# A block of the first layer's out projection for token half 0 set between half 1's products and its last rows, with gate and y rows moved four tiles at a time

## The chip, the core and the metric

The kernel runs on one core of one Trainium2 chip. The metric is device time in microseconds, as a median of several executions. PE is the matrix engine (TensorE), DVE, ACT and POOL are the vector, scalar and GpSimd engines, and SP is the engine that here issues every DMA, one after the other, from one queue. Each engine works through its own list in order; waits between engines go through semaphores.

## What is computed

Two decoder layers over 1024 tokens of width 1024 with 16 heads of 64. The first mixes with forgetting attention (FoX), the second with dilated windows. Cut to what bears on the change:

```python
for i in range(2):
    h = rms_norm(x, norm_g[i])
    if i == 0:
        o, gate = fox_mixer(h, w_in, b_f, q_g, k_g)
    else:
        o, gate = dsw_mixer(h, cos, sin, w_in, q_g, k_g)
    x = x + (o * silu(gate)) @ w_out
```

`fox_mixer` projects `h` to q, k, v, gate and forget logits, and runs causal softmax attention with the running sum of the log forget gates added to the scores. `cos` and `sin` are the rotary tables of the second layer.

## The kernel before

Every large product is made of three fp16 products (high by high, high by low, low by high), so operands exist as a high and a low part: `xh`, `xl` for the normed rows, and in the same buffers `yh`, `yl` for the gated attention output.

**The FoX stage.** After the first layer's gates (`gates`, stored row by row in DRAM as `gs_d`) come eight head pairs, `hp` 0 to 7. For each, `project` (L694) makes q, k and v of eight token tiles `t`, and `fox_tile` queues for every tile: scores on PE (L870), a biased minimum on DVE (L1125), exp on ACT (L913), a low part on POOL (L919), a transposing DMA from `ph` to `ptt` (L920), and the products with v on PE (`pv`, L927 to L929). At a tile's end DVE multiplies by the reciprocal sum and by the gate: two instructions (L1158) that read the gate slice `gsf`, loaded by its own 64 KB DMA for each tile (L1106), and write the tile `y`. For `hp` 0 to 6 a DMA writes `y` to `y_d` (L1162). For the last pair `turn_last` transposes `y` on PE right away (L729), and ACT and DVE split the result into `yh` and `yl` (L734, L735). The rows of the earlier pairs come back from `y_d` in the last pair's time and are turned by `turn_y`.

**The out projection.** `project_t` (L719) multiplies by `w_out` with the weights stationary and 512 tokens (a token half `b`) moving. The 1024 output columns are cut into three weight blocks `h` of 384, 256 and 384 columns, that is 3, 2 and 3 output blocks `m` of 128. One output block takes 24 products: 8 row blocks `k` by 3. For `h` = 0 the order over `k` is 0 to 3, then 4 to 6, then 7, over all three `m`, since `k` = 7 is the last head pair, whose rows come late. The order is: both halves of `h` = 0, then half 0 with `h` = 1 and 2, then half 1 with `h` = 1 and 2. Output blocks wait in three PSUM buffers of `ps_pj` (tile `pj`); three others (`ps_s`, tag `s`) hold scores and transposes.

**What follows an output block.** `grown` loads the old rows (`xr`, L1239), adds the product on DVE (L1241, which frees the PSUM buffer), writes the sum to `x1_d` (L1242), scales by the next norm's gain on ACT (L1244), writes that to `xn_d` (L1245), and adds the squares up (L1247 to L1254). After the eighth block of a half, `factors` makes the row factor: a product `so` on PE (L1262), then `fv` and `fy` on DVE and ACT. `take` loads the rows again (`xs`, L1272); DVE multiplies by `fy` (L1275), ACT casts to `xh` (L1279), and DVE or POOL makes `xl` (L1280). The second layer's gates (`gates`, `project` at L694) read `xh` and `xl`, half 0 first; they load the next weights through `Weights` (`raw`, L619; bound L629 and L631; scale from the product `ws`, L601; split L659 and L660).

**What sets the order.** `Flow` counts ticks as products are written and calls what is due. Then `order_engines` plans all engines' lists from estimated durations and fixes each list; an engine never leaves its list. So a small edit can move instructions in places that it doesn't name. Tiles of one tag share a set number of buffers (`CFG`): `n2k` has 3, for `xr`, the gates' `ge` and a few others, `gsl` 3, `qs` 5. `rotary_tables` (L531 to L570, on DVE and ACT) is due 14 ticks after the first `project_t`.

Of the kernel before, what the change touches and what calls it, by code (L numbers as in the profile page):

```python
# [11 lines left out]
F32 = mybir.dt.float32  # L12
# [5 lines left out]
ALU = mybir.AluOpType  # L18
# [419 lines left out]
def trunk(ctx, tc, ins, out, cfg):  # L438
# [31 lines left out]
    def lay(shape, dtype, name, tag):  # L470
        return layer["pool"].tile(shape, dtype, name=name, tag=tag, bufs=layer["bufs"][tag])
# [138 lines left out]
    class Weights:  # L610
# [87 lines left out]

    def project_t(seq, done):

        under["ps"] = None
        todo = []
        for b, h in seq:
            n = PARTS[h][1] // P
            ms = [[m] for m in range(n)] if h else [list(range(n))]
            for mm in ms:
                for ks in [range(KT)] if h else [range(4), range(4, KT - 1), range(KT - 1, KT)]:
                    todo.extend((b, h, m, k) for m in mm for k in ks)
        n, s0 = 4 * NT * len({h for _, h in seq}), flow.now
        ps, ws = {}, {}  # L710
        for i, (b, h, m, k) in enumerate(todo):
            if h == 0:
                assert all((t, (k > 3) + (k > 6)) in turned for t in range(4 * b, 4 * b + 4)), (b, k, turned)
            if h not in ws:
                ws[h] = next_block(*cfg["out"][len(seq) > 2, len(ws)])
            if k == 0:
                ps[m] = ps_pj.tile([P, 512], F32, name="pj", tag="pj")
            for x, (j, a) in enumerate(((0, yh), (0, yl), (1, yh))):
                nc.tensor.matmul(ps[m], ws[h].slab(k, j)[:, m * P : (m + 1) * P], a[:, k, 512 * b : 512 * (b + 1)], start=(k == 0 and x == 0), stop=(k == KT - 1 and x == 2))  # L719
# [365 lines left out]
    def load_bc(hp, h, es=(0, 1)):  # L1085
        for e in es:
            bcs[hp, e, h] = lay([P, 5 * P], F32, name="bc", tag="ga")
            nc.sync.dma_start(bcs[hp, e, h][:, P:], c_d[2 * hp + e, h * 512 : (h + 1) * 512].partition_broadcast(P))

    def fox_tile(hp, t, kts, vt, sl):  # L1090
        LP = cfg["lpf"]
# [60 lines left out]
        def finish():  # L1152
            o = st["o"]
            rec = sm.tile([P, 2], F32, name="rec", tag="rec")
            nc.vector.reciprocal(rec, o[:, :, HD])
            y = sb.tile([P, P], F32, name="y", tag="y")
            for e in range(2):
                nc.vector.scalar_tensor_tensor(y[:, e * HD : (e + 1) * HD], o[:, e, :HD], rec[:, e : e + 1], st["gs"][:, e * HD : (e + 1) * HD], ALU.mult, ALU.mult)  # L1158
            if hp == NHP - 1:
                turn_last(y, t, flow.now + 3, 0)  # L1160
            else:
                nc.sync.dma_start(y_d[t * P : (t + 1) * P, hp * P : (hp + 1) * P], y)  # L1162


# [346 lines left out]

CFG = dict(out={(False, 0): (), (True, 0): ((18, 20, 22, 24), (0, 0, 1, 1), 3, (4, 6, 8, 10)), (True, 1): ((18, 20, 22, 24), (14, 15, 17, 18), 24, (33, 35, 37, 39))}, take=(((33, 34, 37, 40), 42), ((62, 63, 66, 69), 71)), rush=2000, gate=(((6, 7, 8, 9), (0, 0, 1, 1), 4, (5, 6, 7, 9)), ((44, 45, 46, 47), (26, 28, 30, 32), 36, (38, 40, 42, 44)), ()), bc=((1, 0, 26), (1, 1, 28), (0, 0, 38), (0, 1, 46)), wpool=3, rbufs=8, most=(0, 2), lcm=7, ps=0, pv=100, ph_=100, ph=1, wbufs=8, pl=3, um=3, lpf=8, lsd=((16, 16), (16, 14), (14, 11)), ty2=((0, 4), (1, 5)), hb=2, ub=2, qb=1, nb=3, fox=(((0, 0, 2, 2), (2, 4)), ((0, 0), (4, 4))), due=(29, 33, 39, 45, 35, 41, 49, 57), l1=dict(ga=8, ptt=4, ph=3, p=4, qk_t=6, qs=5, vt=3, gsl=3), l2=dict(ga=4, cmb=4, gsd=4, ptt=3, ph=3, p=2, qk_t=3, og=3, vt=3, gsl=3, par=1), wload=(18, 20, 22, 24), wbound=(0, 1, 3, 4), wscale=8, wsplit=(10, 16, 22, 12))

# [51 lines left out]
```

## Time and profile before

| what | value |
|---|---|
| median of 3 runs | 1655.86 us (1652.52 to 1656.51) |
| profiled execution | 1656.83 us, of which the span is 1654.8 us |
| FoX, first score read by DVE to last y | 142.4 to 531.4 us |
| first layer's out projection | 479.2 to 591.9 us, between other work up to 532 us |
| second layer's gates begin | 591.87 us |

A row of the timeline gives start, duration, engine, line, operation, output and inputs; in brackets stands how long the engine had been idle before it, and who released it. A row of the waits gives who waited for whom, the sum in us, how often, and the longest. A row of the windows gives a stretch, its length, busy time and instructions of each engine, then the granted PE clock as a share of full speed, the share of DMA time, and GB/s.

### The profile page before, as it was taken

To read this page: it belongs to the slowest core of one execution; us is meant where nothing else is said; L and a number is where in the kernel's file an instruction comes from. 1 tells how busy PE (TensorE), PEld (TensorE's weight loads), DVE (VectorE), ACT (ScalarE), POOL (GpSimd) and SP (SyncE) were. 2 spreads that over 40 slices of the span, in tenths; PEclk is the share of its full clock that TensorE was granted. 3 is DMA by queue.
4 is the path that set the end of the run, shared out by engine and by line. 5 is a ranking of instruction groups with operands and counts; after the bars stand their busy time and mean duration, and the time that the engine had idled before them with its cause. 6 is when DMAs were issued, how large, how long until landed. Compare 5 with 4: busy or idle time off the path is not lost.

```text
span 1654.8 us, 37873 instructions
## 1 busy us (share of the span) xinstructions
PE 1605.9 (97%) x13342; PEld 1037.5 (63%) x13342; DVE 1192.6 (72%) x3663; ACT 1063.5 (64%) x2746; POOL 963.9 (58%) x1252
## 2 busy tenths in 40 slices
PE   6999999999998999999999999999999999999999
PEld 4766667777664456566666666666666666666644
DVE  7757878888786586576767787777677877768751
ACT  7656778878776476566766687566566665666630
POOL 7315778778765241255555666667576766858430
PEclk9999999999999999999999999999999999999999
DMA  7335999999999884257876796768787586767952
GB/s 257 127 107 121 205 205 216 203 208 197 206 220 218 237 250 153 85 138 151 168 150 149 164 227 147 174 158 181 160 164 165 141 191 155 170 160 167 219 166 96
DMA packets 646479, 288.66 MB, mean 174 GB/s; under 512 B 493825, under 2 KB 610561, under 8 KB 646289
## 3 DMA queue, kind: packets, MB, share of 16 engines
q1 hardware_dynamic: 646288, 286.25, 74.5%
q8 instruction: 104, 1.70, 0.4%
q14 instruction: 87, 0.70, 0.1%
HBM read 124.35 MB, written 41.22 MB: 100 GB/s over the span
## 4 chain that ended last, share of the span: by engine, by line
PE 74%; DVE 10%; DMA 6%; ACT 4%; issue 3%; POOL 2%; SPq 0%; DVEq 0%; POOLq 0%; ACTq 0%
PE pj L694 56%; PE pj L719 7%; PE s L870 6%; DMA qk_t<-hl 3%; DVE w L660 2%; DVE p L1125 1%; PE ob L929 1%; PE ob L927 1%; PE ob L928 1%; DMA ptt<-ph 1%; ACT w L659 1%; PE o L929 1%; PE o L927 1%; PE o L928 1%; DVE xl L1280 1%
## 5 line engine op out<-in xcount | busy, mean ns | idle before, releaser
L694 PE MATMUL pj<-w,xh 128*128 128x384 f16 (+2 forms) x4864 | 1172.9, 324 | 6.0 <-DVE peak L904 4.3
L694 PE MATMUL pj<-w,xl 128*128 128x384 f16 (+2 forms) x2432 | 787.8, 324 | 5.2 <-DVE xl L1280 3.6
L694 PEld LDWEIGHTS <-xh 128*128 128x128 f16 x4864 | 468.1, 98 | 282.2 <-issue 8.2
L694 PEld LDWEIGHTS <-xl 128*128 128x128 f16 x2432 | 238.2, 98 | 157.5 <-DVE xl L1280 5.3
L1363 POOL TENSOR_TENSOR ph<-p,ph 128x768 f16<-128x768 f32 (+2 forms) x96 | 157.7, 1642 | 137.6 <-ACT ph L1362 130.1
L919 POOL TENSOR_TENSOR ph<-p,ph 128x512 f16<-128x512 f32 (+3 forms) x176 | 173.0, 1003 | 56.9 <-issue 37.5
L837 POOL TENSOR_TENSOR hl<-u,hl 128x512 f16<-128x512 f32 x128 | 150.9, 1179 | 53.6 <-ACT hl L836 44.9
L719 PE MATMUL pj<-xh,w 128*128 128x512 f16 x512 | 157.7, 381 | 6.2 <-DVE xr L1241 2.8
L870 PE MATMUL s<-qk_t 128*128 128x128 f16 (+1 forms) x1248 | 151.2, 238 | 6.8 <-DMA qk_t<-hl 5.1
L660 DVE SCALAR_TENSOR_TENSOR w<-raw,sws,w 128x768 f16<-128x768 f32 x96 | 146.6, 1528 | 11.0 <-ACT w L659 10.7
L794 ACT ACTIVATE sq<-pj 128x256 f32<-128x256 f32 x256 | 96.4, 377 | 86.5 <-DVE u L789 85.7
L789 DVE TENSOR_TENSOR u<-pj,gr 128x256 f32<-128x256 f32 x256 | 106.9, 418 | 45.8 <-PE pj L694 44.0
L913 ACT ACTIVATE p<-p,acc 128x512 f32<-128x512 f32 (+2 forms) x192 | 110.0, 608 | 38.0 <-DVE acc L1125 37.5
L719 PEld LDWEIGHTS <-w 128*128 128x128 f16 x768 | 74.5, 98 | 89.5 <-issue 9.2
L1352 ACT ACTIVATE p<-p,og 128x128 f32<-128x128 f32 (+1 forms) x256 | 104.1, 442 | 27.3 <-DVE og L1350 26.2
L927 PEld LDWEIGHTS <-ptt 128*128 128x128 f16 x1136 | 105.9, 98 | 19.8 <-DMA ptt<-ph 7.9
L928 PEld LDWEIGHTS <-ptt 128*128 128x128 f16 x1136 | 105.2, 96 | 11.4
L629 ACT ACTIVATE jk<-raw 128x768 f16<-128x768 f32 (+2 forms) x88 | 72.2, 820 | 62.5 <-DMA raw<-in_w_dsw 38.7
L821 POOL TENSOR_TENSOR ra<-u,cs 128x128 f32<-128x128 f32 x96 | 44.8, 467 | 108.5 <-DVE u L789 106.6
L1350 DVE CUSTOM_DVE_ANT_0 p<-s,band 128x256 f32<-128x256 f32 (+1 forms) x256 | 90.7, 373 | 22.8 <-PE s L870 22.6
L836 ACT CAST hl<-u 128x512 f16<-128x512 f32 x128 | 78.7, 614 | 42.5 <-DVE u L834 40.2
L929 PEld LDWEIGHTS <-ptt 128*128 128x128 f16 x1136 | 105.4, 97 | 0.0
(211 smaller groups left out, 3017.1 us busy)
## 6 DMA issues: line engine op xcount, KB each, us to landing
raw<-in_w_dsw SPq DMA_DIRECT2D x96, 384.0 KB, 4.2
raw<-in_w_fox SPq DMA_DIRECT2D x32, 384.0 KB, 4.1
og_d<-og SPq DMA_DIRECT2D x64, 132.0 KB, 2.5
cmb<-og_d SPq DMA_DIRECT2D x64, 132.0 KB, 2.9
bc<-c_d SPq DMA_DIRECT2D x32, 256.0 KB, 4.2
gs_d<-ge SPq DMA_DIRECT2D x32, 192.0 KB, 2.2
xt<-in_xt SPq DMA_DIRECT2D x16, 256.0 KB, 3.7
gsf<-gs_d SPq DMA_DIRECT2D x64, 64.0 KB, 2.5
```

Of the source, the lines that this page charges most:

```text
L660: nc.vector.scalar_tensor_tensor(w[:, 1, :, :n], raw, self.sw, w[:, 0, :, :n], ALU.mult, ALU.subtract)
L694: nc.tensor.matmul(ps[:, :n], a[:, k, cols], w.slab(k, j), start=(k == 0 and i == 0), stop=(k == KT - 1 and i == 2))
L719: nc.tensor.matmul(ps[m], ws[h].slab(k, j)[:, m * P : (m + 1) * P], a[:, k, 512 * b : 512 * (b + 1)], start=(k == 0 and x == 0), stop=(k = ...
L789: nc.vector.tensor_mul(u[:, t % 2].rearrange("p (a b) d -> p a b d", a=2), ps[:, : 4 * HD].rearrange("p (a b d) -> p a b d", a=2, b=2), gr ...
L837: nc.gpsimd.tensor_sub(hl[:, :, :4, 1], u, hl[:, :, :4, 0])
L870: nc.tensor.matmul(s[:, c0 : c0 + cnt * P].rearrange("p (c s) -> p c s", c=cnt), q, kk[:, j : j + cnt, e], start=(h == 0), stop=(h == 1), ...
L913: nc.scalar.activation(p, p, AF.Exp, bias=acc, scale=-1.0)
L919: (nc.gpsimd if pool_l else nc.vector).tensor_sub(ph[:, e, 1, cols], p, ph[:, e, 0, cols])
L927: nc.tensor.matmul(o[:, e, :], hi, vt[:, j, e, HD:], start=(b == 0), stop=False, skip_group_check=True)
L928: nc.tensor.matmul(o[:, e, :HD], hi, vt[:, j, e, :HD], start=False, stop=False, skip_group_check=True)
L929: nc.tensor.matmul(o[:, e, :], lo, vt[:, j, e, HD:], start=False, stop=(b == n - 1), skip_group_check=True)
L1363: nc.gpsimd.tensor_sub(ph[:, 1], st["p"], ph[:, 0])
```

## The change

`project_t` now takes a list of units (half, weight block, output blocks, range of `k`), can be called in pieces that share their PSUM tiles, and the units of half 0's block `h` = 1 are put between the three passes of half 1's block `h` = 0:

```diff
-    project_t([(0, 0), (1, 0)], grown)
+    held = {}, {}
+    project_t([(0, 0, range(3), k) for k in CUTS] + [(1, 0, range(3), CUTS[0])], grown, cfg["out"][:1], 24, held, 1)
+    project_t([(0, 1, [0], range(KT)), (1, 0, range(3), CUTS[1]), (0, 1, [1], range(KT)), (1, 0, range(3), CUTS[2])], grown, cfg["out"][1:2], 13, held, 1)
     s0 = flow.now
-    flow.at(s0 + 14, rotary_tables)
+    flow.at(s0, rotary_tables)
...
-    project_t([(0, 1), (0, 2), (1, 1), (1, 2)], grown)
+    project_t([(b, h, [m], range(KT)) for b, h in ((0, 2), (1, 1), (1, 2)) for m in range(PARTS[h][1] // P)], grown, cfg["out"][2:], 51, held)
```

The tiles of that moved block are taken from the scores' PSUM buffers, and all others from `ps_pj` as before:

```diff
+                ps[h, m] = (ps_s.tile([P, 512], F32, name="pj", tag="s") if h == first > 0 else ps_pj.tile([P, 512], F32, name="pj", tag="pj"))
```

The gate slices of four tiles come with one DMA, into a tile of tag `n2k`; y is written in place over them, and for head pairs 0 to 5 four tiles leave with one DMA:

```diff
+    rows4 = {}
+
+    def four(d, hp, h):
+        return d.rearrange("(h j p) c -> h p j c", j=4, p=P)[h][:, :, hp * P : (hp + 1) * P]
...
-                gs = st["gs"] = lay([P, P], F32, name="gsf", tag="gsl")
-                nc.sync.dma_start(gs, gs_d[t * P : (t + 1) * P, hp * P : (hp + 1) * P])
+                if (hp, t // 4) not in rows4:
+                    gs = rows4[hp, t // 4] = [sb.tile([P, 4, P], F32, name="gsf", tag="n2k", bufs=cfg["nb"]), 0]
+                    nc.sync.dma_start(gs[0], four(gs_d, hp, t // 4))
...
-            y = sb.tile([P, P], F32, name="y", tag="y")
+            ys = rows4[hp, t // 4]
+            y = ys[0][:, t % 4]
...
             if hp == NHP - 1:
                 turn_last(y, t, flow.now + 3, 0)
-            else:
+            elif hp == NHP - 2:
                 nc.sync.dma_start(y_d[t * P : (t + 1) * P, hp * P : (hp + 1) * P], y)
+            elif ys[1] == 4:
+                nc.sync.dma_start(four(y_d, hp, t // 4), ys[0])
```

In `CFG`, `n2k` goes from 3 to 4 buffers, `qs` from 5 to 6, the first layer's `gsl` goes away, and the slots of `take` go down by 13 ticks, by which the later start of the last `project_t` call is made good. No product is added or taken away. From the middle of the second layer's gates on, every engine's list is the same in both kernels.

**PE, at the last head pair's last tile.** `pt` is the transpose of the last tile's y; `w_7789` before and `w_7626` now are the weights of `h` = 0 for `k` = 6 and 7, `w_8763` those of `h` = 1. Before:

```order
L929 MATMUL o_9291<-vt_7432,ptt_9136 128x65
L729 MATMUL pt_9375<-ident_88,y_9357 128x128
L601 LDWEIGHTS ones_b_119
L601 MATMUL ws_9444<-vb_9442,ones_b_119 128x4
L719 LDWEIGHTS w_7789
L719 MATMUL pj_9159<-xh_101,w_7789 128x512
```

Now (L715 and L725 are the old L719 and L729):

```order
L715 LDWEIGHTS w_7626
L715 MATMUL pj_9086<-xh_101,w_7626 128x512
L725 MATMUL pt_9219<-ident_88,gsf_8437 128x128
L715 LDWEIGHTS w_8763
L715 MATMUL pj_9254<-xh_101,w_8763 128x512
L715 LDWEIGHTS w_8763
```

Before, the last products with v, the transpose, and the `k` = 7 products that need it follow each other. Now the `k` = 6 products of half 1 stand ahead of the transpose, and 24 products of half 0 behind it; the nine `k` = 7 products come after those. Another 24 products of half 0 stand ahead of half 1's `k` = 4 to 6.

**DVE, at the same place.** `w` are the three splits of the weights of `h` = 2 that DVE makes, `xr` the sums that free PSUM. Before:

```order
L660 SCALAR_TENSOR_TENSOR w_9456<-raw_9199,ws_f_9441,w_9456 128x768
L660 SCALAR_TENSOR_TENSOR w_9468<-raw_9235,ws_f_9441,w_9468 128x768
L660 SCALAR_TENSOR_TENSOR w_9487<-raw_9276,ws_f_9441,w_9487 128x768
L1241 SCALAR_TENSOR_TENSOR xr_9388<-pj_9159,ws_f_7666,xr_9388 128x512
L1241 SCALAR_TENSOR_TENSOR xr_9399<-pj_9209,ws_f_7666,xr_9399 128x512
L1241 SCALAR_TENSOR_TENSOR xr_9411<-pj_9281,ws_f_7666,xr_9411 128x512
```

Now (L1162 is the old L1158, L1248 the old L1241; `pj_9126` and `pj_9254` are the two blocks of `h` = 1, `pj_8966` the first of half 1):

```order
L660 SCALAR_TENSOR_TENSOR w_9201<-raw_9005,ws_f_9183,w_9201 128x768
L1162 SCALAR_TENSOR_TENSOR gsf_8437<-o_9096,rec_9173,gsf_8437 128x64
L660 SCALAR_TENSOR_TENSOR w_9229<-raw_9041,ws_f_9183,w_9229 128x768
L1162 SCALAR_TENSOR_TENSOR gsf_8437<-o_9096,rec_9173,gsf_8437 128x64
L1248 SCALAR_TENSOR_TENSOR xr_9207<-pj_9126,ws_f_8669,xr_9207 128x512
L660 SCALAR_TENSOR_TENSOR w_9248<-raw_9081,ws_f_9183,w_9248 128x768
L731 SCALAR_TENSOR_TENSOR xl_102<-pt_9219,sy_111,xh_101 128x128
L1248 SCALAR_TENSOR_TENSOR xr_9283<-pj_9254,ws_f_8669,xr_9283 128x512
L1248 SCALAR_TENSOR_TENSOR xr_9295<-pj_8966,ws_f_7506,xr_9295 128x512
```

The splits stood between the last transpose and the sums of half 1; now two of them stand among the last tile's y instructions, and all three are ahead of the transpose's low part.

**DVE, from the product `so` of half 0 to the row factor `fy`.** Before:

```order
L1265 TENSOR_SCALAR fv_9719<-so_9717 128x512
L1241 SCALAR_TENSOR_TENSOR xr_9807<-pj_9766,ws_f_8856,xr_9807 128x512
L741 TENSOR_TENSOR fv_9720<-fy_9721 128x512
L742 SCALAR_TENSOR_TENSOR fv_9720<-fv_9720,fv_9719 128x512
L743 SCALAR_TENSOR_TENSOR fy_9721<-fv_9720,fy_9721 128x512
```

Now:

```order
L1272 TENSOR_SCALAR fv_9523<-so_9521 128x512
L737 TENSOR_TENSOR fv_9524<-fy_9525 128x512
L631 TENSOR_REDUCE vm_9771<-raw_9516 128x1
L738 SCALAR_TENSOR_TENSOR fv_9524<-fv_9524,fv_9523 128x512
L1248 SCALAR_TENSOR_TENSOR xr_9675<-pj_9624,ws_f_9183,xr_9675 128x512
L739 SCALAR_TENSOR_TENSOR fy_9525<-fv_9524,fy_9525 128x512
```

A weight bound (L631) has moved in between, and another `xr` sum. On PE, `so` stood 68 products ahead of the second layer's first gate product; now it stands 55 ahead.

More of the change, by code (lines that the diff above doesn't have):

```diff
@@ L667, in slab @@
             return self.pairs[k // 2][:, j, k % 2, : self.n]
+    CUTS = range(4), range(4, KT - 1), range(KT - 1, KT)
     order = [(hp, 0) for hp in range(NHP)] + [(hp, g) for hp in range(NHP) for g in (2, 1)]
@@ L697, in project, with project_t @@
         return ps
-    def project_t(seq, done):
+    def project_t(units, done, keys=((),), ticks=32, held=None, first=0):
         under["ps"] = None
[L702 to L710, printed above, removed]
+        todo = [(b, h, m, k) for b, h, ms, ks in units for m in ms for k in ks]
+        n, s0 = ticks, flow.now
+        ps, ws = held or ({}, {})
+        keys = list(keys)
         for i, (b, h, m, k) in enumerate(todo):
@@ L714, in project_t @@
             if h not in ws:
-                ws[h] = next_block(*cfg["out"][len(seq) > 2, len(ws)])
+                ws[h] = next_block(*keys.pop(0))
             if k == 0:
-                ps[m] = ps_pj.tile([P, 512], F32, name="pj", tag="pj")
+                ps[h, m] = (ps_s.tile([P, 512], F32, name="pj", tag="s") if h == first > 0 else ps_pj.tile([P, 512], F32, name="pj", tag="pj"))
             for x, (j, a) in enumerate(((0, yh), (0, yl), (1, yh))):
-                nc.tensor.matmul(ps[m], ws[h].slab(k, j)[:, m * P : (m + 1) * P], a[:, k, 512 * b : 512 * (b + 1)], start=(k == 0 and x == 0), stop=(k == KT - 1 and x == 2))
+                nc.tensor.matmul(ps[h, m], ws[h].slab(k, j)[:, m * P : (m + 1) * P], a[:, k, 512 * b : 512 * (b + 1)], start=(k == 0 and x == 0), stop=(k == KT - 1 and x == 2))
             if k == KT - 1:
-                done(b, PARTS[h][0] // P + m, ps[m], ws[h].inv)
+                done(b, PARTS[h][0] // P + m, ps[h, m], ws[h].inv)
             while (flow.now - s0) * len(todo) < n * (i + 1):
@@ L1505, in trunk @@
     for h in range(len(PARTS)):
-        project_t([(0, h), (1, h)], finished)
+        project_t([(b, h, ms, k) for b in range(2) for ms, k in ([([m], range(KT)) for m in range(PARTS[h][1] // P)] if h else [(range(3), k) for k in CUTS])], finished)
     flow.drain()
@@ L1509, in trunk @@
     layer["cm"].__exit__(None, None, None)
[L1512 removed]
+CFG = dict(out=((), ((18, 20, 22, 24), (0, 0, 1, 1), 3, (4, 6, 8, 10)), ((18, 20, 22, 24), (14, 15, 17, 18), 24, (33, 35, 37, 39))), take=(((20, 21, 24, 27), 29), ((49, 50, 53, 56), 58)), rush=2000, gate=(((6, 7, 8, 9), (0, 0, 1, 1), 4, (5, 6, 7, 9)), ((44, 45, 46, 47), (26, 28, 30, 32), 36, (38, 40, 42, 44)), ()), bc=((1, 0, 26), (1, 1, 28), (0, 0, 38), (0, 1, 46)), wpool=3, rbufs=8, most=(0, 2), lcm=7, ps=0, pv=100, ph_=100, ph=1, wbufs=8, pl=3, um=3, lpf=8, lsd=((16, 16), (16, 14), (14, 11)), ty2=((0, 4), (1, 5)), hb=2, ub=2, qb=1, nb=4, fox=(((0, 0, 2, 2), (2, 4)), ((0, 0), (4, 4))), due=(29, 33, 39, 45, 35, 41, 49, 57), l1=dict(ga=8, ptt=4, ph=3, p=4, qk_t=6, qs=6, vt=3), l2=dict(ga=4, cmb=4, gsd=4, ptt=3, ph=3, p=2, qk_t=3, og=3, vt=3, gsl=3, par=1), wload=(18, 20, 22, 24), wbound=(0, 1, 3, 4), wscale=8, wsplit=(10, 16, 22, 12))
 def host_layout(inputs):
```

4 lines of the change are left out of this document (3 added, 1 removed).

## The prediction, made before the changed kernel was run

> **What bounds the kernel.** I read the page first, then the waits of PE, then windows and timeline around the out projection.
>
> ```profile
> span 1654.8 us, 37873 instructions
> ...
> PE 1605.9 (97%) x13342; PEld 1037.5 (63%) x13342; DVE 1192.6 (72%) x3663; ACT 1063.5 (64%) x2746; POOL 963.9 (58%) x1252
> ```
>
> PE is the bound: it idles 1654.8 - 1605.9 = 48.9 us in all, and the change removes none of its work. A gain can only come out of those 48.9 us or out of half-clock time. From the middle of the second layer's gates on, all lists are the same, so only the stretch up to about 650 us counts. PE's waits from 470 to 650 us:
>
> ```profile
> PE pt L729 <- DVE y L1158: 4.0, 2, 3.2
> PE pj L694 <- DVE xl L1280: 3.6, 3, 2.0
> PE pj L719 <- DVE xr L1241: 2.8, 1, 2.8
> PE pj L694 <- DVE peak L904: 2.1, 2, 1.3
> ```
>
> ```profile
> 475.00:500.00 25.00, 23.23 (x221) 15.03 (x218) 17.60 (x57) 18.80 (x42) 16.50 (x22) 1.00 1.10 198
> 500.00:525.00 25.00, 22.98 (x264) 15.19 (x265) 17.94 (x48) 17.65 (x34) 14.73 (x14) 1.00 1.01 238
> 525.00:550.00 25.00, 20.12 (x106) 9.04 (x105) 8.57 (x19) 10.64 (x19) 8.10 (x7) 0.93 0.78 213
> 550.00:575.00 25.00, 25.00 (x118) 11.32 (x117) 16.59 (x51) 11.30 (x20) 4.94 (x5) 1.00 0.84 251
> 575.00:600.00 25.00, 22.31 (x106) 10.46 (x105) 24.26 (x24) 17.93 (x26) 16.72 (x10) 0.98 0.85 254
> 600.00:625.00 25.00, 24.19 (x170) 16.87 (x168) 20.65 (x43) 19.38 (x34) 7.77 (x6) 0.95 0.80 237
> ```
>
> Three places lose time: before 502 us (a y), 529 to 541 us (the last tile and PSUM), and from 592 us on (the gates' start). From 575 to 600 us DVE is busy 24.26 of 25 us: there the row factor and `xl` are DVE's chain, and PE waits for it. Of the three numbers at a row's end the first is the granted clock, the second DMA's share.
>
> **The block of half 0 (likeliest term: -5.6 us).** PE's timeline:
>
> ```profile
> 501.82 0.30 PE L729 MATMUL pt<-ident,y 128*128 128x128 f32 x1 [3.16 <-DVE y L1158]
> ...
> 530.03 0.20 PE L927 MATMUL o<-vt,ptt 128*128 128x65 f16 x1 [0.74 <-DMA ptt<-ph]
> ...
> 530.75 0.20 PE L929 MATMUL o<-vt,ptt 128*128 128x65 f16 x1
> 531.81 0.30 PE L729 MATMUL pt<-ident,y 128*128 128x128 f32 x1 [0.87 <-DVE y L1158]
> 531.95 0.17 PE L601 MATMUL ws<-vb,ones_b 128*128 128x4 bf16 x1
> 532.56 0.81 PE L719 MATMUL pj<-xh,w 128*128 128x512 f16 x3 [0.45 <-ACT xh L734]
> ...
> 537.50 0.52 PE L719 MATMUL pj<-xh,w 128*128 128x512 f16 x1 [2.83 <-DVE xr L1241]
> ```
>
> DVE in the same stretch:
>
> ```profile
> 499.18 0.29 DVE L850 TENSOR_SCALAR qs<-qk_t 64x256 int32<-64x256 int32 x1 [2.28 <-DMA qk_t<-hl]
> 500.41 0.28 DVE L1158 SCALAR_TENSOR_TENSOR y<-o,rec,gsf 128x64 f32<-128x64 f32 x1 [0.94 <-DMA gsf<-gs_d]
> ...
> 533.91 2.88 DVE L660 SCALAR_TENSOR_TENSOR w<-raw,ws_f,w 128x768 f16<-128x768 f32 x3 [0.42 <-ACT w L659]
> 536.70 2.06 DVE L1241 SCALAR_TENSOR_TENSOR xr<-pj,ws_f,xr 128x512 f32<-128x512 f32 x3
> ```
>
> The last tile costs 0.74 + 0.87 + 0.45 us, and the next PSUM buffer 2.83 us: `xr` stands behind three weight splits (2.88 us) in DVE's list. Sum 4.9 us. The clock column of 525 to 550 us is 0.93, so 0.07 x 25 = 1.7 us more went at half clock behind these waits. The change puts 24 products ahead of half 1's `k` = 4 to 6 and 24 behind the last transpose. A product takes 0.216 us: between `so`'s end and the gates' start (rows below, 577.2 to 591.87 us) PE makes 68 in 14.7 us. Each block is 5.2 us of cover, more than any of these waits, and the splits are no longer between the last products of half 1 and their `xr`. I take all 4.9 and the 1.7 as gone.
>
> One wait is new. The last transpose needs y, and two splits now stand among y's instructions in DVE's list, each 2.88 / 3 = 0.96 us. From the end of the first moved block on: the scale product `ws` comes 13 products later, at 2.8 us; the first split can start 2.0 us behind it (531.95 to 533.91 us before), at 4.8; with the reciprocal, split, y, split, y (0.28 us each) the last y is done at about 7.5. PE has 27 products (5.8 us) and 24 with v (530.03 to 530.75 us, 0.7 us), so it is there at 6.6. Bounds: 0, if `ws` is early, and 2.9 us, if PE sits through three splits. I take +1.0, the walk's value. Who is queued behind it: the block's 24 products, since PE keeps its order. Then -4.9 - 1.7 + 1.0 = -5.6.
>
> In the Trainium skill, "TensorE: Matmul & The Clock Gate", section "Why this matters for your kernels" says that PE falls back to half clock after idle gaps of about 3 us or more. By that rule the 2.83 us wait would have cost no clock, the 3.16 us wait before 501.82 us would have, and this term would be 3.9 instead of 5.6 us. This trace reads otherwise: the clock is 1.00 in both windows around 502 us, while 0.07 is missing behind waits that are each shorter but lie close together, so I keep 1.7.
>
> **The four-tile gate slice (-2.0).** The 3.16 us wait ends with y, which DVE made only after `qk_t` (499.18 us) and then `gsf` (500.41 us) had come. With one load for four tiles `gsf` is there long before, and in the new list y stands ahead of the wait for `qk_t`. What is late next is `qk_t` itself and the transposes `ptt`: scores need `qs`, at the earliest about 499.8 us, and PE has roughly 1 us of other work from 498.7 us on. Bounds 0 and -3.2; I take -2.0.
>
> **84 DMAs fewer (-1.0).** 48 loads of `gsf` and 36 writes of y go; the bytes stay.
>
> ```profile
> gsf<-gs_d SPq DMA_DIRECT2D x64, 64.0 KB, 2.5
> ```
>
> ```profile
> PE o L927 <- DMA ptt<-ph: 4.1, 4, 1.5
> ```
>
> ```profile
> SPq L1162 <- DVE y L1158: 5.0, 7, 1.4
> ```
>
> PE waits only 4.1 us for `ptt` from 140 to 440 us, so at most 4.1 us is to be had, whatever SP saves; PE's other work hides the rest. Below nothing: SP stood 5.0 us for y before, up to 1.4 us at a time, and a four-tile write waits for its last tile. Ordinary bounds -4.1 and +1.5 (one such wait shown to PE). I take -1.0.
>
> **The rotary tables** keep their distance to half 0's end: the new call's start lies 13 ticks later, they move up by 14. They need DVE, which from 550 to 575 us is busy 16.59 of 25 us and whose waits hide under PE's products. No term; if that cover went, it would show in the next one.
>
> **The gates' start (+3.3).**
>
> ```profile
> 576.33 1.02 PE L1262 MATMUL so<-sacc,ones 128*128 128x512 f32 x2
> ...
> 591.87 0.49 PE L694 MATMUL pj<-w,xh 128*128 128x384 f16 x2
> ...
> 594.04 0.34 PE L694 MATMUL pj<-w,xl 128*128 128x384 f16 x1 [0.71 <-DVE xl L1280]
> ...
> 598.47 0.34 PE L694 MATMUL pj<-w,xl 128*128 128x384 f16 x1 [1.98 <-DVE xl L1280]
> ...
> 624.68 0.48 PE L694 MATMUL pj<-w,xh 128*128 128x384 f16 x2 [0.77 <-DVE peak L904]
> ...
> 629.09 0.34 PE L694 MATMUL pj<-w,xl 128*128 128x384 f16 x1 [0.95 <-DVE xl L1280]
> ...
> 631.20 0.48 PE L694 MATMUL pj<-w,xh 128*128 128x384 f16 x2 [1.29 <-DVE peak L904]
> ```
>
> From `so` at 576.33 us DVE's chain takes 22.1 us until the gates' products run on at 598.47 us. `so` now stands 55 instead of 68 products ahead of the gates: PE arrives 13 x 0.216 = 2.8 us earlier against the same chain, and waits that much longer. To the chain come a bound and one more `xr`:
>
> ```profile
> 598.31 0.69 DVE L631 TENSOR_REDUCE vm<-raw 128x1 f32<-128x512 f32 x1
> ```
>
> ```profile
> 593.91 0.72 DVE L1241 SCALAR_TENSOR_TENSOR xr<-pj,ws_f,xr 128x512 f32<-128x512 f32 x1
> ```
>
> 0.69 + 0.72 = 1.4 us, of which the bound stood in the chain's last part already. Half clock (0.02 and 0.05 x 25 us, 1.7 us here) runs beside these waits in part. Bounds: 0, if the chain runs faster with fewer `xr` sums colliding, and +7.6, the whole of the two gains; I take 2.8 + 0.5 = +3.3.
>
> **Later gates (-0.5).** The waits at 624.68, 629.09 and 631.20 us are 3.0 us; half 1's rows come from a chain that starts when half 1 ends, and PE is held up at the start, so some may go. Bounds 0 and -3.0; I take -0.5.
>
> **Sum**, against the profiled execution: 1656.83 - 5.6 - 2.0 - 1.0 + 3.3 - 0.5 = 1651.0 us. That execution is 1.0 us above the median of the runs (1655.86), so the forecast is 1650.0 us, -0.35%. About 0.3%, 5 us here, is what a measurement of this kernel can tell from no change.
>
> **The rivals.**
>
> *The PSUM wait stays.* The first block of half 0's `h` = 2 needs a buffer that half 1's `xr` frees. Those rows' loads stand in SP's queue behind the write of `xg` of the first moved block, and so behind two splits and an `xr`. SP's list speaks for it; by the walk above they are issued about 10.2 us after the first moved block's end and needed at 13.9. Against it speaks that these 3.7 us are just over the median of such a load from 475 to 545 us, the last number here:
>
> ```profile
> xr<-in_xp SPq DMA_DIRECT2D x7, 256.0 KB, 3.4
> ```
>
> If they come late, 2.8 and 1.7 us return: 1650.0 + 4.5 = 1654.5 us. Chance 0.18.
>
> *The gates take all back.* If DVE's chain starts from times that don't move with PE (loads of the gate weights, the tables), PE arrives 7.6 us early and waits them all: 1656.83 - 1.0 - 0.5 - 1.0 = 1654.3 us, about 1654. For it: DVE's 24.26 of 25 us. Against: `ws`, `so` and the sums follow PE's products. Chance 0.13.
>
> *The gates take nothing back.* The sum without 3.3: 1646.7 us. For it: the chain loses its collisions. Against: the 13 products. Chance 0.10.
>
> *Slower: SP stands on the four-tile writes.* SP issues in order, and behind a write that waits for its fourth y stand the transposes that PE's next products need. Twelve such writes at up to 1.4 us would be 16.8 us, if none were hidden; with the other gains 1650 + 1 + 16.8 = about 1668 us. It decides once more than 10 of the 16.8 us show on PE. Against it: PE waited only 4.1 us for transposes with 56 writes of one tile in SP's list. Chance 0.07.
>
> That the block doesn't do what it says is excluded by the lists: the 48 products stand where they should.
>
> **How the numbers follow.** The forecast's own case has 0.52 and spans 1647 to 1653 us; 1650.9 us and below counts as faster, some 0.65 of it. Faster: 0.52 x 0.65 + 0.10 = 0.44, and 0.02 from the edges of the others: 0.46. Slower: 0.07. Same: 0.47. The range goes from 1645 us, which holds the third rival with some room, to 1657 us, which holds the first two and a loss in the DMA term; what it leaves out is the slower case and edges, under 0.2.
>
> **What would show it.** PE's row at the first product of `h` = 2 has no wait for `xr`, and the clock there stays at 1.00; the last transpose waits about 1 us for y; the wait of 3.16 us is under 1.5. At the gates' start the waits for `xl` sum to some 5 to 6 us, where they were 2.7. The forecast is wrong if `ptt` waits in the FoX stage grow, if the gates' first wait swallows over 6 us, or if PE waits for `xr` loads.

## The result, and the profile after

The changed kernel takes 1645.09 us (median of 6 runs, 1643.78 to 1648.36); the kernel before, in runs on the same chip, takes 1654.70 us (6 runs). The ratio is 0.9943, with a 95% interval from 0.9927 to 0.9960. Run once more on another chip (`after_again` below) it is 0.9914, 0.9885 to 0.9943. So the change is faster by 0.4 to 1.15%; the forecast was 0.35%, and 1645.09 us lies 0.1 us inside the lower edge of its range (1645 to 1657).

The head of the page of the changed kernel:

```profile
span 1643.1 us, 37739 instructions
...
PE 1601.4 (97%) x13342; PEld 1036.0 (63%) x13342; DVE 1199.4 (73%) x3663; ACT 1061.3 (65%) x2746; POOL 961.0 (58%) x1252
```

PE is idle 41.7 us instead of 48.9, and busy 4.5 us less (1605.9 before) with the same products. Of that, 1.7 us is the half clock from 525 to 550 us, where the granted clock goes from 0.93 to 1.00; what the rest is stays open. The waits of PE from 470 to 650 us, the stretch that the prediction looked at (who waited for whom, sum, times, longest):

```profile
PE pj L695 <- DVE xl L1287: 2.7, 3, 1.7
PE pj L695 <- DVE xr L1248: 2.3, 1, 2.3
PE pj L695 <- DVE peak L900: 1.6, 3, 1.0
PE so L1269 <- DVE sacc L1261: 1.6, 1, 1.6
PE s L866 <- DVE xl L731: 1.1, 1, 1.1
```

The 3.2 us for y and the 2.8 us for a PSUM buffer in the out projection are gone; waits of products `pj` with L695 (the second layer's gates) stand at the top, and `so` now waits for `sacc`, the sum of the squares. The same in the windows (stretch, length, busy time of the engines, granted clock, DMA share, GB/s):

```profile
500.00:525.00 25.00, 25.00 (x227) 14.11 (x224) 11.31 (x32) 14.80 (x28) 11.86 (x13) 1.00 0.93 228
525.00:550.00 25.00, 24.32 (x114) 10.85 (x112) 15.40 (x41) 9.31 (x14) 6.72 (x5) 1.00 0.83 247
550.00:575.00 25.00, 23.10 (x106) 10.16 (x105) 14.82 (x32) 14.66 (x28) 6.87 (x7) 1.00 0.86 248
575.00:600.00 25.00, 20.01 (x101) 9.84 (x100) 22.94 (x32) 19.16 (x28) 14.44 (x9) 0.93 0.84 250
```

From 500 to 550 us PE hardly stops, and the clock that was 0.93 from 525 to 550 us is 1.00. The loss has moved to the stretch from 575 us on. PE's timeline, in the places that the prediction named:

```profile
493.94 0.27 PE L866 MATMUL s<-qk_t 128*128 128x256 f16 x1 [1.11 <-DVE xl L731]
...
526.53 0.30 PE L725 MATMUL pt<-ident,gsf 128*128 128x128 f32 x1 [0.64 <-DVE gsf L1162]
...
533.58 0.79 PE L715 MATMUL pj<-xh,w 128*128 128x512 f16 x2
...
565.80 1.13 PE L1269 MATMUL so<-sacc,ones 128*128 128x512 f32 x2 [1.55 <-DVE sacc L1261]
...
578.64 0.49 PE L695 MATMUL pj<-w,xh 128*128 128x384 f16 x2
...
583.56 0.48 PE L695 MATMUL pj<-w,xh 128*128 128x384 f16 x2 [2.31 <-DVE xr L1248]
...
590.46 0.34 PE L695 MATMUL pj<-w,xl 128*128 128x384 f16 x1 [1.72 <-DVE xl L1287]
```

The last transpose waits 0.64 us for its y (which is now written into the tile `gsf`), `h` = 2 starts at 533.58 us without a wait, and the gates begin at 578.64 us. The longest wait there, 2.31 us, is not for `xl` but for a PSUM buffer, which DVE frees with a row sum `xr` of half 1. That sum stands in DVE's list behind two products for half 0's rows:

```profile
579.29 3.56 DVE L1282 TENSOR_TENSOR xs<-xs,fy 128x512 f32<-128x512 f32 x2
582.77 0.74 DVE L1248 SCALAR_TENSOR_TENSOR xr<-pj,ws_f,xr 128x512 f32<-128x512 f32 x1
```

Where the time came from is seen best at fixed points of PE's list. These are starts of products, each read from the PE timeline of one profiled execution; the run `lists of before` (`e5_before_lists`) and the last column (`e11_sines_92`) are explained below:

| start of | before | lists of before, 84 fewer DMAs | changed | tables in the first gates |
|---|---|---|---|---|
| FoX, first score | 141.55 | 141.72 | 141.61 | 140.91 |
| out projection, first product | 479.33 | 473.38 | 472.52 | 472.76 |
| second layer's gates | 591.87 | 584.54 | 578.64 | 578.29 |
| `so` of half 1 | 604.57 | 597.13 | 593.74 | 588.35 |
| last product of the kernel | 1650.76 | 1643.03 | 1638.72 | 1634.26 |

Not all of these profiles come from one chip. The second profile of the changed kernel, on another chip, shows how far such points can differ between two executions: 472.46 us at the out projection, 579.84 us at the gates, 595.29 us at half 1's `so` and 1640.19 us at the last product, so up to 1.6 us.

The changed kernel is 6.8 us ahead before the first product of the out projection, where the block has not begun. It is 13.2 us ahead at the gates, and 10.8 us at half 1's `so`. So two questions were open: why the FoX stage gained nearly seven microseconds, where the prediction had 1.0 for the fewer DMAs, and what takes time back at the gates.

### The profile page after: what moved, and what is told of

It is laid out like the page before. It is cut to its first block, busy times and chain, and to the rows that moved or that the text cites. A ratio compares the mean times of both kernels' runs of the same rounds, so it can differ in the third digit from the quotient of the medians.

```text
span 1643.1 us, 37739 instructions
## 1 busy us (share of the span) xinstructions
PE 1601.4 (97%) x13342; PEld 1036.0 (63%) x13342; DVE 1199.4 (73%) x3663; ACT 1061.3 (65%) x2746; POOL 961.0 (58%) x1252
## 4 chain that ended last, share of the span: by engine, by line
PE 78%; DVE 8%; DMA 5%; ACT 4%; issue 3%; POOL 2%; SPq 0%; DVEq 0%; ACTq 0%; POOLq 0%
PE pj L695 60%; PE s L866 6%; PE pj L715 6%; DMA qk_t<-hl 2%; DVE w L660 2%; PE ob L925 1%; PE ob L923 1%; PE ob L924 1%; PE o L925 1%; PE o L923 1%; PE o L924 1%; DMA raw<-in_w_gate 1%; ACT w L659 1%; DVE xs L1282 1%; DVE p L1127 1%
## 5 line engine op out<-in xcount | busy, mean ns | idle before, releaser
L695 PE MATMUL pj<-w,xh 128*128 128x384 f16 (+2 forms) x4864 | 1172.0, 324 | 7.3 <-DVE xr L1248 2.3
L695 PE MATMUL pj<-w,xl 128*128 128x384 f16 (+2 forms) x2432 | 788.3, 324 | 3.2 <-DVE xl L1287 2.7
L695 PEld LDWEIGHTS <-xh 128*128 128x128 f16 x4864 | 467.4, 98 | 283.2 <-issue 7.8
L695 PEld LDWEIGHTS <-xl 128*128 128x128 f16 x2432 | 238.0, 98 | 156.8 <-DVE xl L1287 5.0
L715 PE MATMUL pj<-xh,w 128*128 128x512 f16 x512 | 156.9, 379 | 2.6 <-DVE xr L1511 2.5
L660 DVE SCALAR_TENSOR_TENSOR w<-raw,sws,w 128x768 f16<-128x768 f32 x96 | 150.2, 1566 | 9.5 <-ACT w L659 9.2
L715 PEld LDWEIGHTS <-w 128*128 128x128 f16 x768 | 73.7, 98 | 84.8 <-issue 4.2
```

The costliest lines, as they stand in the source:

```text
L660: nc.vector.scalar_tensor_tensor(w[:, 1, :, :n], raw, self.sw, w[:, 0, :, :n], ALU.mult, ALU.subtract)
L695: nc.tensor.matmul(ps[:, :n], a[:, k, cols], w.slab(k, j), start=(k == 0 and i == 0), stop=(k == KT - 1 and i == 2))
L715: nc.tensor.matmul(ps[h, m], ws[h].slab(k, j)[:, m * P : (m + 1) * P], a[:, k, 512 * b : 512 * (b + 1)], start=(k == 0 and x == 0), stop=( ...
```

## The experiments

Theory A was that the 84 fewer DMAs bring the FoX stage's gain; its rivals were the block (B) and other lists of the planner (C). Ratios are to the kernel before on the same chip; each group of runs had a chip of its own.

**Each part alone.** The first run adds only the four-tile slices (with their buffers) to the kernel before, the second only the block with its slots and tables.

```diff
 e1_four_only: the kernel before, and
+    rows4 = {}
+    def four(d, hp, h): ...
-nb=3, ... qs=5, vt=3, gsl=3
+nb=4, ... qs=6, vt=3
 e2_block_only: the changed kernel, and
+                gs = st["gs"] = lay([P, P], F32, name="gsf", tag="gsl")
+                nc.sync.dma_start(gs, gs_d[t * P : (t + 1) * P, hp * P : (hp + 1) * P])
-nb=4, ... qs=6, vt=3
+nb=3, ... qs=5, vt=3, gsl=3
```

> The kernel before with the gate slices and y by four tiles (n2k with 4 buffers, qs with 6, as in the changed kernel), and the out projection, the take slots and the tables as before. Theory A (the term of the 84 DMAs was too small, the whole FoX stage runs closer): 6 to 8 us faster than before (ratio 0.995 to 0.996), first out-projection product at about 472.5 us of the profile (479.3 before), PE's waits for ptt under 2 us (4.9 before). Theory B (the DMA term is about 1 us as predicted and the block of half 0 brought the rest): 2 to 4 us faster (0.9975 to 0.999), first product at 476 us or later. In both, the waits of 0.74, 0.87, 0.45 and 2.83 us from 529 to 541 us stay, shifted.

> The changed kernel with the gate slices and y tile by tile as before (n2k with 3 buffers, qs with 5, the old pools): the block of half 0, the take slots and the tables alone. Theory A: the block's 5.6 us less the 3.3 us given back at the gates' start, 2 to 4 us faster than before (ratio 0.9975 to 0.999), first out-projection product at 478 to 480 us as before. Theory B: 5 to 7 us faster (0.9955 to 0.997), gates' start waits no longer than before (2.7 us).

The slices alone: 1652.35 us against 1659.84, ratio 0.9958 (0.9945 to 0.9971), first product of the out projection at 473.83 us. The block alone: 1660.74 us, ratio 1.0001 (0.9986 to 1.0016), first product at 479.13 us. Theory A holds for the slices. For the block even its 2 to 4 us were too much: its lead of 2.9 us at the gates' start is gone at half 1's `so` (605.27 us, 604.57 before), and in its out projection PE still stands 2.27 us for a PSUM buffer (at 577.04 us, for `xr`).

**Loads or writes.** Two runs put a part of the DMAs back into the changed kernel.

```diff
 e4_y_single
-            elif hp == NHP - 2:
+            else:
                 nc.sync.dma_start(y_d[t * P : (t + 1) * P, hp * P : (hp + 1) * P], y)
-            elif ys[1] == 4:
-                nc.sync.dma_start(four(y_d, hp, t // 4), ys[0])
 e6_gsf_single
-                    nc.sync.dma_start(gs[0], four(gs_d, hp, t // 4))
+                nc.sync.dma_start(rows4[hp, t // 4][0][:, t % 4], gs_d[t * P : (t + 1) * P, hp * P : (hp + 1) * P])
```

> The changed kernel with y written tile by tile again (36 more writes), the gate slices still loaded by four tiles. If the gain in the FoX stage comes from the loads (gsf there early, 48 fewer loads), this is within 1.5 us of the changed kernel (ratio to before 0.994 to 0.9955) and the first out-projection product stays at 472 to 474 us. If it comes from SP not standing on the writes of y, 3 us or more return (0.996 to 0.998), and PE's waits for ptt are back at 3 us or more.

> The changed kernel with the gate slices loaded tile by tile (48 more loads) into the same four-tile buffer; y is still written by four tiles. If the loads carry the gain, 3 us or more return (ratio to before 0.996 to 0.998) and the wait of a transpose for y ahead of the last tiles (3.16 us before) is back at over 1 us. If the writes carry it, it is within 1.5 us of the changed kernel (0.994 to 0.9955).

Both lose nearly all, more than either side of their expectations had allowed: 0.9996 (0.9985 to 1.0007) with single writes, 0.9987 (0.9979 to 0.9996) with single loads. But these runs don't show what a DMA costs. The planner that sets every engine's list counts the DMAs, and with other DMAs it makes other lists for the whole FoX stage. In e4 a wait appears that neither kernel has, for the rows `yt` that are loaded back behind the writes of y:

```profile
487.29 0.87 PE L725 MATMUL pt<-ident,yt 128*128 128x128 f32 x3 [3.81 <-DMA yt<-y_d]
```

**The same lists, other DMAs.** So the next three runs hold every engine's list fixed. The order is written into the kernel as numbers, in place of the planner:

```diff
-    for line in plan_engines(steps, *step_graph(steps, book.rows)).values():
+    for line in lines:   # lines: the order that the planner gave for another kernel
```

`e5_before_lists` runs the 84 fewer DMAs in the lists of the kernel before, `e6_after_lists` 84 more in the lists of the changed kernel, `e7_e4_lists` the four-tile DMAs in the lists of e4. The changed kernel itself ran with them.

> The kernel before with the gate slices and y by four tiles (84 fewer DMAs), but every engine's list held to the one that the planner made for the kernel before: PE, DVE, ACT and POOL run word for word the same order, SP's list has a four-tile load where the first of its four stood and a four-tile write where the last stood. Theory A (fewer DMAs in themselves bring the FoX stage's gain): 5 to 8 us faster than before (ratio 0.995 to 0.997), first out-projection product 5 to 7 us earlier. Theory C (the gain comes from the other lists that the planner makes once it counts 84 fewer DMAs): within 2 us of before (0.999 to 1.001), first product at 477 to 480 us, the waits for ptt still 3 us or more.

> The changed kernel with 84 DMAs more (each four-tile load and write issued as four of one tile, one behind the other at the same place in SP's list), and every engine's list held to that of the changed kernel. Theory A: 5 to 9 us slower than the changed kernel (ratio to before 0.998 to 1.000), waits for ptt and qk_t grow by 5 us. Theory C: within 2 us of the changed kernel (0.993 to 0.996), first out-projection product at 472 to 474 us.

> The changed kernel (all loads and writes by four tiles) with every engine's list held to the one that the planner made for the run with single writes of y (e4_y_single, ratio 0.9996); a four-tile write stands where the last of its four stood. Theory A (the 36 writes themselves cost e4 its gain): as fast as the changed kernel, 0.993 to 0.996. Theory C (e4 lost by its lists): as slow as e4, 0.998 to 1.0005, with the wait of about 3.8 us of a transpose for yt behind the first out-projection products.

> The changed kernel once more, on the same chip and against the same runs of before as the three others: 0.993 to 0.996 by both theories. If it lies above 0.997 here, the comparison with the four runs before has to be read with that.

| run | median, us | ratio to before | 95% interval |
|---|---|---|---|
| e5_before_lists | 1651.06 | 0.9945 | 0.9922 to 0.9968 |
| e6_after_lists | 1660.90 | 1.0000 | 0.9985 to 1.0015 |
| e7_e4_lists | 1656.50 | 0.9974 | 0.9960 to 0.9989 |
| after_again | 1647.40 | 0.9914 | 0.9885 to 0.9943 |

The changed kernel itself came out faster than its expected 0.993 to 0.996 here, so the chips differ in what the change brings, or the noise is wider than one group of runs shows.

The number of DMAs decides, in both directions: with the lists held, 84 fewer bring 0.55%, and 84 more cost the changed kernel all that it had gained. e5 also has the changed kernel's buffers (`n2k` 4, `qs` 6), so alone it would not tell the DMAs from the buffers; e6 has the same buffers as the changed kernel and differs from it in the DMAs only. In e6 the four DMAs stand one behind the other, not spread as in the kernel before, so its loss is the price of that arrangement. The FoX stage in one window, 150 to 475 us, of the kernel before, of e5, of the changed kernel and of e6, in this order (the second number is PE's busy time):

```profile
150.00:475.00 325.00, 317.09 (x3481) 226.85 (x3479) 270.95 (x884) 250.74 (x620) 253.84 (x312) 1.00 0.99 204
```

```profile
150.00:475.00 325.00, 322.48 (x3539) 231.53 (x3537) 278.01 (x899) 256.14 (x630) 259.28 (x316) 1.00 0.99 208
```

```profile
150.00:475.00 325.00, 322.65 (x3544) 232.18 (x3543) 283.11 (x899) 256.53 (x632) 258.71 (x317) 1.00 1.00 209
```

```profile
150.00:475.00 325.00, 315.38 (x3436) 223.51 (x3435) 274.75 (x874) 247.38 (x612) 250.33 (x308) 1.00 0.94 201
```

With 84 DMAs fewer PE stands 5.4 us less (e5 against before), with 84 more 7.3 us longer (e6 against the changed kernel). The clock is 1.00 in all four, and the DMA share and the GB/s are, if anything, higher with fewer DMAs. What differs is SP's time. The same write of y, on SP's queue, of the changed kernel and of e6:

```profile
200.33 0.53 SPq L1169 DMA_DIRECT2D y_d<-gsf  x1
201.40 8.97 SPq L916 DMA_TRANSPOSE ptt<-ph  x4
```

```profile
201.73 2.35 SPq L1179 DMA_DIRECT2D y_d<-gsf  x4
204.19 7.95 SPq L924 DMA_TRANSPOSE ptt<-ph  x4
```

Four tiles in one DMA take 0.53 us of SP, in four DMAs 2.35 us, and the transposes stand behind them. In e6 PE's waits for `ptt` from 150 to 480 us are 5.7 us, in the changed kernel 0.4. Two more readings point the same way. From 150 to 475 us SP is issuing for 282.0 us in the kernel before and 269.8 in e6, but for 245.8 in e5 and 244.8 in the changed kernel (sums of SP's rows). And once a transpose is issued, fewer DMAs don't make it land sooner: the median from issue to landing of `ptt` in this window is 4.3 us before, 4.2 in e5, 4.2 in the changed kernel and 3.9 in e6. That SP's time for issuing is the way in which the DMAs cost is thus likely. No run issued them from another queue, so it is not shown by an experiment.

The Trainium skill, "DMA: Bandwidth & Descriptors", section "Issuing engines are not separate DMA queues", says that the time to initiate a DMA is usually small relative to the DMA itself. For one DMA this trace agrees (0.43 us of SP, and 2.5 us to landing, the medians for `gsf` before). The runs show that the sum can still decide, where one queue carries everything.

The lists matter too: e7 has as few DMAs as the changed kernel and is 9 us slower, with the wait for `yt` of e4 (3.52 us at 488.29 us). Its 0.9974 lies between what the two theories had expected. So of what e4 lost, 0.82% against the changed kernel, the 36 writes would be about 0.22% and the lists the rest; the chips were not the same, and the intervals of e4 and e7 overlap, so the 0.22% is not clear of noise.

**The tables.** The gates' start was the second question. ACT's timeline of the changed kernel, while half 0's rows are finished (`nsq` are the squares that `so` sums):

```profile
539.61 0.63 ACT L1257 ACTIVATE nsq<-xr 128x512 f32<-128x512 f32 x1 [0.27 <-DMA xn_d<-xg]
540.25 1.28 ACT L564 ACT_TABLE_LOAD   x1
552.03 0.36 ACT L564 ACTIVATE sn<-rt 128x192 f32<-128x192 f32 x1 [10.50 <-DVE rt L554]
...
557.19 0.61 ACT L1257 ACTIVATE nsq<-xr 128x512 f32<-128x512 f32 x1
...
559.14 0.61 ACT L1257 ACTIVATE nsq<-xr 128x512 f32<-128x512 f32 x1
...
564.34 0.61 ACT L1257 ACTIVATE nsq<-xr 128x512 f32<-128x512 f32 x1
```

ACT loads the table of sines at 540.25 us and then stands 10.5 us for the angles `rt`, which DVE makes between other work. The squares of half 0's last three rows stand behind it, and `so` comes at 565.80 us, 11.0 us after DVE's last `xr` of half 0 starts (554.80 us). The stop is not all that holds the third square. It also stands behind a weight split `w`, before which ACT was idle 3.13 us for the scale `ws_f`. DVE made that scale only after it had stood 5.70 us for a row load:

```profile
561.42 0.75 DVE L1248 SCALAR_TENSOR_TENSOR xr<-pj,ws_f,xr 128x512 f32<-128x512 f32 x1 [5.70 <-DMA xr<-in_xp]
...
562.89 0.94 ACT L659 ACTIVATE w<-raw,ws_f 128x768 f16<-128x768 f32 x1 [3.13 <-issue]
```

The stop has a part in this too: the scale comes from a bound `vm` that ACT finishes at 556.48 us, behind the sines. The kernel before has the same stop, 9.15 us, and the block alone (e2) a longer one, 15.33 us, with a wait of 4.35 us for PE at the gates; that the one makes the other is not shown. ACT of before, ACT of e2, PE of e2:

```profile
562.33 0.36 ACT L564 ACTIVATE sn<-rt 128x192 f32<-128x192 f32 x1 [9.15 <-DVE rt L554]
```

```profile
567.31 0.36 ACT L564 ACTIVATE sn<-rt 128x192 f32<-128x192 f32 x1 [15.33 <-DVE rt L554]
```

```profile
593.81 0.50 PE L695 MATMUL pj<-w,xl 128*128 128x384 f16 x1 [4.35 <-DVE xl L1276]
```

Theory D says that this stop sets the gates' start. Two runs move the tables: back to the distance before, and into the second layer's gates. Up to the out projection the lists of PE, DVE and ACT are those of the changed kernel.

```diff
-    flow.at(s0, rotary_tables)
+    flow.at(s0 + 14, rotary_tables)     # e8_tables_14
+    flow.at(s0 + 84, rotary_tables)     # e9_tables_84
```

> The changed kernel with the rotary tables 14 ticks later again, at s0 + 14 (the FoX stage's lists are the changed kernel's word for word). In the changed kernel's trace ACT stands 10.5 us before sn (552.03 us) for DVE's chain of rt, and behind it in ACT's list stand xg and nsq of half 0's last tiles, so that so starts at 565.8 us, some 8 us after half 0's last xr. Theory D (the tables' place sets so, and so the gates' start): nsq of half 0 stands ahead of sn here, so starts 2 to 5 us earlier, but fy then stands behind sn; 1 to 3 us faster than the changed kernel at best, ratio to before 0.990 to 0.994. Rival E (moving them up paid, the prediction's zero was too little): 1 to 4 us slower than the changed kernel, 0.994 to 0.997.

> The changed kernel with the rotary tables at s0 + 84, in the middle of the second layer's gates, behind every nsq, fy and split of both halves; the FoX stage's lists are the changed kernel's word for word. Theory D: so starts at 557 to 560 us of the profile (565.8 in the changed kernel), the waits of the gates' start (0.29 + 0.50 + 2.31 + 1.72 = 4.8 us) fall under 2 us, the clock of 575 to 600 us goes back to 1.00; 4 to 7 us faster than the changed kernel, ratio to before 0.988 to 0.991. Rival E (DVE's and POOL's splits bound the gates' start whenever so comes, or the tables' work costs the same in the gates): within 2 us of the changed kernel, 0.991 to 0.9955.

e8: 1652.54 us, ratio 0.9946 (0.9925 to 0.9968). e9: 1655.10 us, 0.9962 (0.9946 to 0.9977). Neither beats the changed kernel, and both miss what theory D expected. e8 lies where rival E put it. Its stop is shorter (7.35 us at 562.06 us), yet `so` comes at 569.21 us, 3.4 us later than in the changed kernel, where 2 to 5 us earlier was expected: two of the three squares now stand ahead of the stop, but the last one, at 567.74 us, still stands behind it. So it is not the length of the stop that counts, but what stands behind it. The waits at the gates' start are longer than the changed kernel's 4.8 us: 6.7 us.

```profile
582.59 1.46 PE L695 MATMUL pj<-w,xh 128*128 128x384 f16 x4 [2.73 <-ACT xh L1286]
585.92 0.50 PE L695 MATMUL pj<-w,xl 128*128 128x384 f16 x1 [1.87 <-DVE xl L1287]
591.50 0.34 PE L695 MATMUL pj<-w,xl 128*128 128x384 f16 x1 [2.09 <-DVE xl L1287]
```

In e9 theory D came true at the place it spoke of, and the same stop turned up elsewhere. PE of e9, then its ACT:

```profile
558.60 1.02 PE L1269 MATMUL so<-sacc,ones 128*128 128x512 f32 x2
...
632.80 0.80 PE L695 MATMUL pj<-w,xh 128*128 128x384 f16 x2 [11.41 <-DVE peak L900]
```

```profile
626.32 0.36 ACT L564 ACTIVATE sn<-rt 128x192 f32<-128x192 f32 x1 [11.56 <-DVE rt L554]
```

`so` is 7.2 us earlier, 3.6 us after DVE's last `xr` of half 0 starts (554.96 us) instead of 11.0; the waits at the gates' start are 1.3 us (0.29 and 1.01) instead of 4.8, the clock from 575 to 600 us is 1.00, and half 1's `so` starts at 587.42 us instead of 593.74. Then ACT stands 11.56 us for the angles in the middle of the gates, and PE stands as long for what ACT has not done.

So the last two runs split the tables: the angles first, straight into the tiles `sn` and `cs`, the sines when the angles are done, both in the first layer's gates, where DVE is busy 11.83 and ACT 11.73 of 25 us (100 to 125 us of the changed kernel).

```diff
-    flow.at(s0, rotary_tables)
+    flow.at(flow.now + 60, rotary_angles)   # ahead of gates(0, ...)
+    flow.at(flow.now + 76, rotary_sines)    # e10_tables_first_gates
+    flow.at(flow.now + 92, rotary_sines)    # e11_sines_92, in place of 76
```

> The changed kernel with the tables split in two and moved into the first layer's gates: DVE's chain for the angles at tick 60 of those gates (100 to 125 us of the changed kernel's profile, DVE busy 11.8 and ACT 11.7 of 25 us), the three sines at tick 76, when the angles are done; the angles stand in the tiles sn and cs themselves. The FoX stage's lists stay the changed kernel's. Theory D (so is late because ACT stands for the tables' chain at the out projection; the 11.41 us wait for peak in e9_tables_84 was the same stop in another place): so at 557 to 560 us, waits at the gates' start under 2 us, the clock of 575 to 600 us at 1.00, and no wait over 3 us for peak; 4 to 8 us faster than the changed kernel, ratio to before 0.986 to 0.991. Rival E (what so gains is lost again in the gates by DVE's and POOL's splits, or the first gates lose as much to the sines): within 2 us of the changed kernel, 0.991 to 0.9955.

> The run before (e10_tables_first_gates) with the three sines at tick 92 of the first layer's gates instead of 76, so that ACT comes to them some 10 us after DVE has the angles (99.74 us there). Theory D (a stop of ACT for DVE's chain is the cost, wherever it stands): the wait of 3.49 us for peak at 105.07 us and the half clock of 100 to 125 us (0.93, 1.75 us) go, first scores at 141.5 us as in the changed kernel (146.88 in e10); so at 557 to 560 us, second so at 587 to 590 us; 5 us faster than e10, ratio to before 0.987 to 0.990, 4 to 7 us faster than the changed kernel. Rival F (the sines' 4 us on ACT and two table loads cost PE the same wherever they stand in the gates): first scores still at 145 us or later, ratio 0.991 to 0.993.

e10: 1643.52 us, ratio 0.9920 (0.9901 to 0.9939). By the ratio alone this lies in rival E's range. The waits at the gates' start are about as in e9 (1.4 us) and no long wait follows, but ACT came to the sines 3.08 us ahead of the angles, and PE paid at once, at half clock behind it (0.66 from 105 to 110 us): the first FoX score starts at 146.88 us instead of 141.61. PE of e10, and its window:

```profile
105.07 0.48 PE L699 MATMUL pj<-w,xh 128*128 128x384 f16 x2 [3.49 <-DVE peak L904]
```

```profile
105.00:110.00 5.00, 4.93 (x21) 2.55 (x21) 4.13 (x9) 4.49 (x9) 1.64 (x1) 0.66 0.53 172
```

e11: 1642.83 us, ratio 0.9897 (0.9880 to 0.9913). ACT of e11 does the sines without a wait, PE does not stop near them, and `so` comes at 559.30 us:

```profile
107.93 1.28 ACT L570 ACT_TABLE_LOAD   x1
109.23 0.36 ACT L570 ACTIVATE sn<-sn 128x192 f32<-128x192 f32 x1
```

```profile
559.30 1.02 PE L1275 MATMUL so<-sacc,ones 128*128 128x512 f32 x2
```

In the first gates theory D is shown: e10 and e11 differ in the sines' tick alone, and with the stop go the 3.49 us, the half clock and the late first score (140.91 us), while the sines stay. What costs there is ACT standing for DVE's angles, and not the sines. At the out projection the runs take away the stop, the sines and DVE's work for the angles together; that it is the stop which costs is read there from ACT's list. e11 is the fastest kernel here: its profiled span is 1639.0 us, against 1643.1 and 1644.5 us of the changed kernel in two profiles. Its ratio is the lowest, and its interval lies clear of the changed kernel's first one (0.9927 to 0.9960); with the second (0.9885 to 0.9943) it overlaps, so how much it gains over the changed kernel is not settled by the times alone.

## Why the prediction was right or wrong

The direction held, and the range by 0.1 us; the gain is 1.6 to 2.4 times the forecast (0.57% and 0.86% against 0.35%). That the time still lies in the range is luck: one term was a sixth of what it then measured, and the 0.86% of the second chip, taken off the kernel before (1655.86 us), would give 1641.6 us, below the range. The terms, on the profiled execution (1654.8 to 1643.1 us of span, -11.7):

- **The block of half 0, predicted -5.6: right for the waits that it named.** In e5, where before's order meets the new DMAs, the old waits are still there: 0.67 + 0.87 + 0.45 + 2.83 = 4.8 us, and 0.34 x 5 = 1.7 us of half clock behind the last.

```profile
530.17 0.49 PE L727 MATMUL pj<-xh,w 128*128 128x512 f16 x1 [2.83 <-DVE xr L1260]
```

```profile
530.00:535.00 5.00, 4.83 (x15) 1.90 (x15) 1.44 (x3) 3.62 (x6) 2.25 (x3) 0.66 0.83 251
```

 In the changed kernel 0.64 us are left of it, the last transpose's wait for y (1.0 was predicted). 4.8 + 1.7 - 0.6 = 5.9 us. The rule weighed in the prediction, half clock only behind gaps of about 3 us or more (the Trainium skill, "TensorE: Matmul & The Clock Gate", section "Why this matters for your kernels"), would have left the 1.7 us out; this window shows them behind 2.83 us.
- **The four-tile slice, -2.0: right.** The wait of 3.16 us became one of 1.11 us at 493.94 us.
- **84 DMAs fewer, -1.0: the step that failed.** Measured with the lists held it is -6.0 us up to the first product of the out projection (479.33 to 473.38 us), and 84 more cost 10.3 us there in the changed kernel's lists (472.46 us in `after_again` to 482.76 us). The bound of -4.1 was wrong in its reasoning: it counted only the waits that the view puts down to `ptt`. Four more waits of the stage, for `acc`, `xl`, `u` and `qs` of DVE, 3.6 us from 439 to 472 us, shrank as well, to 1.7 us for DVE. That they did because DVE's chain hangs on transposes too is likely, but not shown. In e5 all waits of the stage together are 2.5 us, 7.7 before.
- **The rotary tables, no term: wrong, and with them the cause given for the gates' start.** The profile of before had the row to read: ACT standing 9.15 us for `rt`. The prediction looked at DVE, which is busy there, and found cover on PE; it did not look at what stands behind the sines in ACT's list.
- **The gates' start, +3.3: right in size, by another way.** The waits are 4.8 us (2.7 before), and `so` waits 1.55 us more: about +3.7 us, and one stretch of half clock as before. The prediction had 5 to 6 us of waits for `xl`; those are 2.0 us, and the longest is the 2.31 us for a PSUM buffer. Nor was the chain from `so` the limit. `so` itself was late, by ACT's stop and the split behind it, and e11 shows the start with 1.3 us of waits.
- **Later gates, -0.5: right.** 2.5 us instead of 3.0.

The sum with the measured terms, -5.9 - 2.0 - 6.0 + 3.7 - 0.5 = -10.7 us, is near the -11.7 of the span. The rivals: PE never waited for a row `xr` at `h` = 2 (DVE did, 4 us at 532.53 us, under the cover of the block's products); the gates took under a third back (3.7 of 13.9 us), not all; SP did not stand on the four-tile writes. With the slices taken out, in e2, the first two rivals have a part: PE waits 2.27 us for a PSUM buffer in the out projection, and the gates take back the 2.9 us that are left.

What stays open is why the block brings nothing alone and some 3 us on top of the slices (e5's span 1647.4 us against 1643.1 and 1644.5, on different chips). e2's stop of ACT is 15.33 us against 10.5; but the lists of the two kernels differ in more than that.

## What to carry to other kernels

Where one queue issues everything, count its instructions as work of an engine: merging DMAs moves the same bytes, but takes less of the queue's time (here 0.53 us for four tiles instead of 2.35), and what stands behind them gains. Read an engine's list at each wait for a rare operation: what cost here was not the operation, but what was queued behind it while its input was made elsewhere, so make the input first and the operation late. Where a planner makes the order, one edit changes all lists, so an experiment that undoes the edit measures the new lists too; hold the order fixed to see the edit alone.

## What the runs showed of the hardware

A plain DMA takes SP 0.43 us for 64 KB and 0.53 us for 256 KB (medians for `gsf`), so the size hardly counts there. Gaps of PE of 1.98 us (e5, 591.03 us), 2.83 and 3.49 us were each followed by a 5 us window at a clock of 0.66 or 0.67, that is about 1.7 us lost for each, where the prediction had spread one loss over several close waits; the gap of 3.16 us before 501.82 us in the kernel before was followed by none, and so was its gap of 1.95 us before 1599.18 us. The length of a gap alone does not decide.
